# Sum of two weight blocks made by accumulating DMAs instead of VectorE, in a one-core encoder kernel

## The chip, the cores and the metric

The kernel runs on one core of one Trainium2 chip. The core has a matrix engine (TensorE, "PE" in the profile), a vector engine (VectorE, "DVE"), a scalar engine (ScalarE, "ACT"), a general engine (GpSimd, "POOL") and a synchronisation engine (SyncE, "SP"). Each of them runs its own list of instructions in order and waits for the others by semaphores. Weights come from DRAM by DMA; a DMA is issued from the queue of SP, ACT or POOL. The metric is the device time of one execution in microseconds; the median of several executions is compared.

## What is computed

A bidirectional encoder trunk of two layers on 512 positions of width 1024, in float32:

```python
for l in range(DEPTH):
    xn = rms_norm(x, ln1[l])
    z = xn @ w_in[l]
    a_q, a_i, a_ff, a_fb, a_g, b_u, b_v, c_q, c_k, c_v, gz = jnp.split(z, offsets, axis=-1)
    ...
    gates = jax.nn.sigmoid(gz.reshape(bsz, s_len, N_BRANCH, D_MODEL))
    merged = (gates[:, :, 0] * (y_a @ w_br[l, 0])
              + gates[:, :, 1] * (y_b @ w_br[l, 1])
              + gates[:, :, 2] * (y_c @ w_br[l, 2]))
    x = x + merged @ w_out[l]
    hn = rms_norm(x, ln2[l])
    x = x + jnp.square(jax.nn.relu(hn @ w_up[l])) @ w_down[l]
return rms_norm(x, final_norm)
```

The three branches are a gated linear recurrence (y_a), a gated spatial mixing (y_b) and a windowed attention (y_c).

## The kernel before

**Split products.** Every float32 matrix product is made of three faster ones. `wsplit` (L201 to L205) casts a weight tile of 128 x 1024 to a rounded high half on ScalarE (`wh`, L203), and takes the remainder on VectorE (`wl`, L204). There are `WB = 3` buffers of each. TensorE then multiplies high by high, high by low and low by high.

**Block units.** Fourteen large products are made by a scheme with seven block products in place of eight. Such a unit multiplies a left operand of 512 x 1024 by weights of 1024 x 1024, both cut in 2 x 2 blocks. Per layer there are three units of the input projection (key `un`, u = 0 to 2: the values of branches A and B, then the gates of branches C and A) and four of the down projection (key `dn`, qd = 0 to 3, between the up projections of the MLP). In order of time they are numbered here from 0: units 0 to 2 are `un` of layer 0, 3 to 6 `dn` of layer 0, 7 to 9 `un` of layer 1, 10 to 13 `dn` of layer 1.

`uload` (L187 to L195) loads a unit's eight weight tiles of 512 KB from SyncE's queue into the eight buffers `wq` (`NQ = 8`), in the order b11, b12, b22, b21, two tiles each. A buffer is loaded again only when the unit before has done with it. The four sums of weight blocks are made in place:

- b12 + b22 in `early_sums` (L417 to L420), on VectorE, ahead of the unit. The result stands in b12's buffers and is called `t3` in the unit. Where a `mark` is given, the additions are not issued before that instruction.
- b11 + t3 at L447, for the products n = 6;
- b11 - b22 at L449, for n = 5;
- b21 + b11 at L451, for n = 4.

`seven` (L422 to L475) runs the products in the order 1, 2, 6, 7, 5, 4, 3 (in unit 7: 1, 7, 6, 2, 5, 4, 3, with four other products between the first two). Product 1 needs b11, 2 needs b21, 6 needs b11 + t3, 7 needs t3 itself, and 3 needs b22. For each product two tiles are split and 24 matmuls of 512 columns run (L433 to L435). Its names in the profile are tA, tB, tC for unit 0 and 7, gA to gC for the gate units, dA to dC for the down projection. The outcomes are taken from PSUM by VectorE and ScalarE (L478 and L841 to L891).

**Order.** The program is written in one order, with priorities (`hp`, `later`). A planner then fixes the list of each engine, by its own times for the instructions. What the list holds is run in order. GpSimd's list holds the reciprocal square roots of the norms (L270, L278, L949), the stores of the gates (`thd`, L874) and of x (`xspill`, L1232), and several loads. The left operands' sums and splits (`left_x`, L407 to L415) and the sums of squares of x (`norm_sums`, L303 to L308) run in unit 0 beside the first products.

**Start.** The first loads are x, the four tiles of `bu` and unit 0's eight tiles, then eight rows of x for `norm_sums` (L777).

Of the kernel before, what the change touches and what calls it, by code (L numbers as in the profile page):

```python
# [9 lines left out]
AF = mybir.ActivationFunctionType  # L10
ALU = mybir.AluOpType
# [22 lines left out]
def _chunk_keys():  # L34

    res = []
    for l in range(DEPTH):

        res += [(l, "bu", i) for i in range(4)]


        res += [(l, "un", u, q, i) for u in range(3) for q in range(4) for i in range(2)]
        for h in range(NH):
            res += [(l, "f", h, 0), (l, "f", h, 1), (l, "q", h)]
        res += [(l, "ck"), (l, "cv")] + [(l, "cq", j) for j in range(4)]
        for d in range(KT):
            res += [(l, "gz", d)] + [(l, "yb", d // 2)] * (d % 2 == 0)
        res += [(l, "ag", h) for h in range(NH)]
        res += [(l, "y", br, fl, i) for br in (2, 0) for fl in range(2) for i in range(2)]
        res += [(l, "wo", fl, i) for fl in range(2) for i in range(4)]  # L50
        for qd in range(4):
            res += [(l, "up", qd, f) for f in range(8)]
            res += [(l, "dn", qd, q, i) for q in range(4) for i in range(2)]
    return res


CHUNK = {k: i for i, k in enumerate(_chunk_keys())}


def trunk(tc, xT, xt, ws, vec, fnb, bsb, snk, wst, rope, cmask, amask, ident, out):  # L60
    nc = tc.nc
# [33 lines left out]
    def nm(s):  # L95
        ctr[0] += 1
        return f"{s}_{ctr[0]}"

    def T(tag, name, dt=F32):
        where = part[HOME[tag]] if tag in HOME else sb  # L100
        return where.tile([P, S], dt, tag=tag, bufs=SLOTS[tag], name=nm(name))

    def begin(which):
        part[which] = pool(name=nm(which), bufs=1)
# [82 lines left out]
    def uload(*key):  # L187

        raw = []
        for i in range(8):  # L190
            t = part["wq"].tile([P, CW], F32, tag="wq", bufs=NQ, name=nm("wq"))
            with hp():
                nc.sync.dma_start(t, ws[CHUNK[key + (i // 2, i % 2)]])
            raw.append(t)
        return [raw[2 * q:2 * q + 2] for q in range(4)]  # L195

    def whl():
        return (sb.tile([P, CW], F32R, tag="wh", bufs=WB, name=nm("wh")),
                sb.tile([P, CW], F32R, tag="wl", bufs=WB, name=nm("wl")))
# [12 lines left out]
    def proj(xs, name, *key, bank="m"):  # L212

        return proj_w(xs, name, wload(*key), bank=bank)
# [88 lines left out]
    def norm_sums(n, xrows):  # L303

        ss = SM("ss8", 8)
        for j, x in enumerate(xrows):
            nc.scalar.activation(T("jk", "jk"), x, AF.Square, scale=D ** -0.5, accum_out=ss[:, j:j + 1])
        n.rc = rstd_d(ss, 0, 4)  # L308
# [94 lines left out]
    def behind(mark):  # L403

        return tc.issue_after(mark.ins) if mark else contextlib.nullcontext()
# [8 lines left out]
            res.append(h)  # L414
        return res  # L415

    def early_sums(raw, mark=None):  # L417
        with behind(mark):
            for b12, b22 in zip(raw[1], raw[2]):
                nc.vector.tensor_tensor(b12, b12, b22, ALU.add)  # L420

    def seven(raw, hs, name, on, order=(1, 2, 6, 7, 5, 4, 3), between=None, apart=False, swap=False):  # L422

# [334 lines left out]
    raw, hi, lo = sb.tile([P, CW], F32, tag="wr", bufs=WR, name=nm("wr")), *whl()  # L758
# [27 lines left out]
    for l in range(DEPTH):  # L786
# [25 lines left out]
        def project_bu():  # L812
            pts = proj_four(xs, "bu", l, "bu", banks="mmcc" if l else "mmaa")
            if l == 0:
                raw = [T("l2", "bu") for _ in pts]
                for t, pt in zip(raw, pts):
                    nc.scalar.copy(t, pt)
                return raw
            norm_rows(n1)
            return [evac(pt, "l2", "bu") for pt in pts]  # L820
# [5 lines left out]
        hx = left_x(n1, lambda: T("xs", "xs", F32R))  # L826
        if l == 0:
            raw = unit0
            early_sums(raw)
            norm_sums(n1, x0r)  # L830
            boost[0] = True
        rc = n1.rc
# [37 lines left out]
        def on_gate(i):  # L870
            w = {}

            def keep(z, t, fl):
                nc.gpsimd.dma_start(thd[:, i * 4 + t, fl * S:(fl + 1) * S], z)  # L874

            def on(which, p, pt):
                A, V = nc.scalar, nc.vector
                if which in ("P1", "P16", "P7"):
                    w[which, p] = T("zt", "zt")
                    kept.append(A.copy(w[which, p], pt))  # L880
                elif which == "P1653":
                    z = T("zt", "zt")
                    A.activation(z, pt, AF.Tanh, scale=sc[:, 4 + p:5 + p])
                    keep(z, p, 1)
                else:
                    z = w.pop(({"P2": "P1", "P165": "P7", "P74": "P16"}[which], p))
                    past.append(V.tensor_tensor(z, z, pt, ALU.add))
                    t, fl, c = {"P2": (p, 0, p), "P165": (2 + p, 1, 6 + p), "P74": (2 + p, 0, 2 + p)}[which]
                    A.activation(z, z, AF.Tanh, scale=sc[:, c:c + 1])
                    keep(z, t, fl)  # L890
            return on  # L891

        for u in range(3):
            nxt = uload(l, "un", u + 1) if u < 2 else None
            if u == 0:
                if l:
                    seven(raw, hx, "t", on_tok, (1, 7, 6, 2, 5, 4, 3), lambda mark: bu.extend(project_bu()), swap=(u + l) % 2)
                else:
                    seven(raw, hx, "t", on_tok, (1, 2, 6, 7, 5, 4, 3), swap=(u + l) % 2)
            else:  # L900
                seven(raw, hx, "g", on_gate(u - 1), between=None if l or u > 1 else rows_behind, swap=(u + l) % 2)
                if l == 0 and u == 1:
                    with behind(kept[0]):
                        for ts in (vt, bv):
                            for i, t in enumerate(ts):
                                nc.scalar.activation(t, t, AF.Copy, scale=rc[:, i:i + 1])
            if nxt:
                early_sums(nxt)
            raw = nxt
        end("G")  # L910
        end("wq")
# [332 lines left out]
        for qd in range(4):  # L1244
            hs, nh = [], [0]

            def new():
                nh[0] += 1
                return T("jk" if nh[0] == 1 else "rb" if nh[0] == 2 else "h", "sh", F32R)

            def keys(j):
                return [(l, "up", qd, 2 * j + i) for i in range(2)]

            early = {j: pair_load(keys(j), True) for j in AHEAD[qd]}
            for j in range(4):
                if j in PAIRS[qd] or j in early:
                    us = up_pair(*(early.get(j) or pair_load(keys(j), False)), hx, "s" if j % 2 else "m")
                for i in range(2):
                    f = 2 * j + i
                    if j in PAIRS[qd] or j in early:  # L1260
                        u = us[i]
                    else:
                        pt = proj(n2.xs, f'up{qd}', l, "up", qd, f, bank="s" if f % 4 > 1 else "m")
                        u = T("z", "u")
                    if f == 0:
                        raw = uload(l, "dn", qd)
                    with hp():
                        if j not in PAIRS[qd] and j not in early:
                            nc.scalar.activation(u, pt, AF.Relu)
                            mark = nc.scalar.activation(u, u, AF.Square)  # L1270
                        if f % 2 == 0:
                            hs.append(left_first(new, u))
                        else:
                            rest = left_second(new, hs[-1], u, f == 7)
                    if f == 3:
                        early_sums(raw, mark)

            def between(mark):
                for part_ in rest:
                    with hp():  # L1280
                        part_(lambda: T("l2", "sh", F32R))

            if qd == 3:
                if last:
                    for fl in range(2):
                        fn_t.append(T("z", "fn"))
                        nc.sync.dma_start(fn_t[fl], bass.AP(tensor=fnb.tensor, offset=fnb.offset + fl * S, ap=[[0, P], [1, S]]))
                else:
                    nxt = uload(l + 1, "un", 0)
            down(qd, raw, hs, xr, r2, nr2, done, between, last)  # L1290
        if not last:
            with hp():
                n1.end()
            raw = nxt
            end("mlp")
            begin("G")
            early_sums(raw)
        xsrc = xspill

    for p in reversed(pools):  # L1300
# [119 lines left out]
```

## Time and profile before

| what | us |
|---|---|
| median of 3 executions | 1645.49 |
| lowest and highest | 1645.30 and 1646.45 |
| profiled execution: its span, first to last instruction | 1644.4 |

For the profiled execution the profile gives the span and no time of its own; what lies around a span is seen by holding it against the median. The mean granted clock of TensorE was 0.999.

How to read the lines below. A group of instructions is shown as line, engine, operation, `written<-read`, shape, `xcount | busy us, mean ns | idle us just before, and what ended it`. In a list of waits each row says who waited for whom, the total, the number of times and the longest. A row of the timeline starts with its start and its duration in us. A table of stretches gives the busy time of each engine in each stretch (with the number of instructions), the granted clock, the share of the 16 DMA engines that was busy, and GB/s. "DMA to landing" is the time from the issue of a DMA to the arrival of its data. An engine's name with a q is its queue: it issues or waits.

### The profile page before, as it was taken

Reading aid. Unit: us, or ns where it says so; the run is one execution under the profiler, and the core shown is the slowest. Engines: PE = TensorE matmul, PEld = TensorE weight load, DVE = VectorE, ACT = ScalarE, POOL = GpSimd, SP = SyncE. Lnnn points to the kernel's source line nnn. Section 1 sums busy time; section 2 is a strip of 40 time slices with the busy share of each in tenths; the row PEclk is TensorE's granted clock in tenths of the full one; section 3 lists DMA queues with packets and bytes.
Section 4 is the critical chain, followed back from the end, with each engine's and each line's share of the span. In section 5 each row is a group of like instructions: output and inputs, shape, how many; then the busy total and the mean of one; then the engine's idle time right before and its main releaser. Section 6 shows DMA issues by size and latency. Waiting matters only on the chain. (4 is left out here: it accounts for less than half of the span.)

```text
span 1644.4 us, 24323 instructions
## 1 busy us (share of the span) xinstructions
PE 1631.2 (99%) x9137; PEld 1376.8 (84%) x9137; DVE 1358.9 (83%) x2183; ACT 1012.9 (62%) x1731; POOL 102.4 (6%) x165
## 2 busy tenths in 40 slices
PE   9999999999999999999999999999999999999998
PEld 7788888888888898989888888888887888989896
DVE  7888979677758988898989869887877589898887
ACT  7667567677247564646666555886862464647374
POOL 0012000000300000000010110000003000000001
PEclk9999999999999999999999999999999999999999
DMA  8343222222625333232423432223226343232311
GB/s 309 102 154 125 78 90 73 102 97 85 236 92 190 100 106 103 103 115 91 141 90 125 144 121 78 77 91 105 92 86 232 106 162 117 89 128 77 129 65 52
DMA packets 55590, 191.55 MB, mean 116 GB/s; under 512 B 7376, under 2 KB 7632, under 8 KB 55472
## 3 DMA queue, kind: packets, MB, share of 16 engines
q1 hardware_dynamic: 44352, 154.43, 27.3%
q0 software_dynamic: 10688, 35.00, 5.8%
q8 instruction: 72, 1.18, 0.3%
q10 hardware_dynamic: 432, 0.55, 0.1%
q14 instruction: 46, 0.38, 0.1%
HBM read 173.18 MB, written 16.78 MB: 116 GB/s over the span
## 5 line engine op out<-in xcount | busy, mean ns | idle before, releaser
L203 ACT CAST wh<-wq 128x1024 fp32r<-128x1024 f32 x214 | 225.2, 1053 | 205.1 <-PE dA L434 60.9
L204 DVE TENSOR_TENSOR wl<-wq,wh 128x1024 fp32r<-128x1024 f32 x214 | 260.4, 1221 | 62.8 <-ACT wh L203 60.3
L203 ACT CAST wh<-wr 128x1024 fp32r<-128x1024 f32 x164 | 172.0, 1049 | 155.1 <-PE wo L251 27.5
L204 DVE TENSOR_TENSOR wl<-wr,wh 128x1024 fp32r<-128x1024 f32 x164 | 199.9, 1220 | 61.0 <-ACT wh L203 55.1
L210 PE MATMUL up<-xh,wl 128*128 128x512 f32 x320 | 124.8, 390 | 0.0
L209 PE MATMUL up<-xl,wh 128*128 128x512 f32 x320 | 124.8, 390 | 0.0
L208 PE MATMUL up<-xh,wh 128*128 128x512 f32 x320 | 124.6, 391 | 0.0
L434 PE MATMUL dA<-wh,sh 128*128 128x512 f32 x256 | 99.8, 390 | 0.0
L433 PE MATMUL dA<-wh,sh 128*128 128x512 f32 x256 | 98.5, 390 | 0.0
L435 PE MATMUL dA<-wl,sh 128*128 128x512 f32 x256 | 91.9, 389 | 0.0
L656 DVE TENSOR_TENSOR ex<-ex 128x512 f32<-128x512 f32 x112 | 74.9, 686 | 3.5 <-ACT kt L647 3.2
L208 PEld LDWEIGHTS up<-xh,wh 128*128 128x128 f32 x320 | 60.1, 188 | 12.4
L210 PEld LDWEIGHTS up<-xh,wl 128*128 128x128 f32 x320 | 60.1, 188 | 12.3
L209 PEld LDWEIGHTS up<-xl,wh 128*128 128x128 f32 x320 | 60.1, 188 | 12.2
L644 ACT ACTIVATE qt<-ex 128x512 f32<-128x512 f32 x56 | 37.9, 677 | 33.8 <-DVE ex L656 31.8
L433 PEld LDWEIGHTS dA<-wh,sh 128*128 128x128 f32 x256 | 48.1, 188 | 10.0
L434 PEld LDWEIGHTS dA<-wh,sh 128*128 128x128 f32 x256 | 48.1, 188 | 9.9
L435 PEld LDWEIGHTS dA<-wl,sh 128*128 128x128 f32 x256 | 48.1, 188 | 9.9
L523 PE MATMUL us<-xs,wh 128*128 128x256 f32 x192 | 54.1, 283 | 0.0
L522 PE MATMUL us<-xs,wh 128*128 128x256 f32 x192 | 54.1, 283 | 0.0
L524 PE MATMUL us<-xs,wl 128*128 128x256 f32 x192 | 53.4, 283 | 0.0
L208 PE MATMUL gz<-xh,wh 128*128 128x512 f32 x128 | 50.9, 398 | 0.0
(435 smaller groups left out, 4780.6 us busy)
## 6 DMA issues: line engine op xcount, KB each, us to landing
wr<-in_ws_dram SPq DMA_DIRECT2D x158, 512.0 KB, 3.5
wq<-in_ws_dram SPq DMA_DIRECT2D x124, 512.0 KB, 4.3
thd<-zt POOLq DMA_DIRECT2D x32, 256.0 KB, 2.5
gt<-thd POOLq DMA_DIRECT2D x32, 256.0 KB, 3.9
mgd<-mg POOLq DMA_DIRECT2D x16, 256.0 KB, 2.3
mB<-mgd POOLq DMA_DIRECT2D x16, 256.0 KB, 6.7
x<-in_xT_dram SPq DMA_DIRECT2D x8, 256.0 KB, 7.5
xt<-in_xt_dram SPq DMA_DIRECT2D x8, 256.0 KB, 8.3
```

The source lines that it names most:

```text
L203: nc.scalar.copy(hi, raw)
L204: nc.vector.tensor_tensor(lo, raw, hi.bitcast(F32), ALU.subtract)
L208: nc.tensor.matmul(pt, whi, xhi, start=first, stop=False)
L209: nc.tensor.matmul(pt, whi, xlo, start=False, stop=False)
L210: nc.tensor.matmul(pt, wlo, xhi, start=False, stop=last)
L433: nc.tensor.matmul(pt, xh[:, t], hi[:, c], start=start and k == 0, stop=False, skip_group_check=True)
L434: nc.tensor.matmul(pt, xl[:, t], hi[:, c], start=False, stop=False, skip_group_check=True)
L435: return nc.tensor.matmul(pt, xh[:, t], lo[:, c], start=False, stop=k == 3, skip_group_check=True)
L522: nc.tensor.matmul(pt, hi[:, c], xh, start=n in (1, 2, 7) and k == 0, stop=False, skip_group_check=True)
L523: nc.tensor.matmul(pt, hi[:, c], xl, start=False, stop=False, skip_group_check=True)
L524: nc.tensor.matmul(pt, lo[:, c], xh, start=False, stop=k == 3, skip_group_check=True)
L656: nc.vector.tensor_tensor(o_ap, o_ap, ap_of(ex, i_, [[istep, 2]] + z), ALU.add)
```

## The change

`early_sums` no longer adds on VectorE. It issues two DMAs from GpSimd's queue, each of which reads a tile of b22 from DRAM and adds it onto the loaded tile of b12. The tiles of b22 are still loaded by `uload` too, since the products 5 and 3 use them. The function now takes the key of the unit in place of a mark; the four calls stay where they were, and the down units' sums have no mark any more. That is 28 instructions of VectorE less and 28 DMAs of 512 KB more.

```diff
-    def early_sums(raw, mark=None):
-        with behind(mark):
-            for b12, b22 in zip(raw[1], raw[2]):
-                nc.vector.tensor_tensor(b12, b12, b22, ALU.add)
+    def early_sums(raw, *key):
+        for i in range(2):
+            nc.gpsimd.dma_start(raw[1][i], ws[CHUNK[key + (2, i)]], accum_op=ALU.add)
...
-            early_sums(raw)
+            early_sums(raw, 0, 'un', 0)
...
-                early_sums(nxt)
+                early_sums(nxt, l, 'un', u + 1)
...
-                            mark = nc.scalar.activation(u, u, AF.Square)
+                            nc.scalar.activation(u, u, AF.Square)
...
-                        early_sums(raw, mark)
+                        early_sums(raw, l, 'dn', qd)
...
-            early_sums(raw)
+            early_sums(raw, l + 1, 'un', 0)
```

## Prediction

> **What bounds the kernel now.** I began with the head of the page, then asked for the waits of TensorE (PE), then for busy time in stretches that I chose around the block units.
>
> ```profile
> span 1644.4 us, 24323 instructions
> PE 1631.2 (99%) x9137; PEld 1376.8 (84%) x9137; DVE 1358.9 (83%) x2183; ACT 1012.9 (62%) x1731; POOL 102.4 (6%) x165
> ```
>
> PE is busy for 1631.2 of 1644.4 us; 13.2 us are left. VectorE (DVE) at 83% is the second engine. What a lighter DVE can give is what PE waits for it:
>
> ```profile
> PE idle L167 <- DVE idle L164: 1.6, 1, 1.6
> PE tA L435 <- DVE wl L204: 1.3, 1, 1.3
> PE wo L251 <- DVE mgl L259: 0.4, 2, 0.3
> PE po L1084 <- ACT sc L1074: 0.4, 1, 0.4
> PE av L728 <- DVE st L712: 0.3, 1, 0.3
> PE tC L435 <- DVE wl L204: 0.3, 1, 0.3
> PE kT L701 <- DVE own L634: 0.3, 1, 0.3
> PE gA L435 <- DVE wl L204: 0.2, 1, 0.2
> PE mT L1159 <- DVE gt L1174: 0.2, 1, 0.2
> ```
>
> Columns: who waited for whom, total, times, longest. The nine sum to 5.0 us. The first, 1.6, is the start of the program. The rows at L435 are inside block units: tA and tC in unit 0 (1.3 + 0.3) and gA in a gate unit (0.2), so 1.8 us in all.
>
> ```profile
> core 0: us, PE busy (x) PEld busy (x) DVE busy (x) ACT busy (x) POOL busy (x), PEclk, DMA share, GB/s
> 10.00:30.00 20.00, 20.00 (x89) 16.35 (x88) 17.62 (x24) 15.03 (x24) 1.79 (x3) 1.00 1.03 414
> 28.20:66.50 38.30, 36.70 (x160) 29.57 (x159) 34.04 (x47) 27.26 (x46) 5.10 (x3) 1.00 0.51 169
> 540.00:579.00 39.00, 39.00 (x174) 32.30 (x173) 34.75 (x44) 18.63 (x22) 0.00 (x0) 1.00 0.36 116
> ```
>
> The last row is a down-projection unit of the MLP: PE 39.00 of 39.00 us at granted clock 1.00, DVE 34.75. DVE is nearly full there, yet PE never stops: relief buys nothing. The row from 28.20 is unit 0: PE lacks 1.6 us of 38.3. The row from 10.00 is the start, where the DMA engines are full (share 1.03, 414 GB/s).
>
> **The change, part by part.** *Removed:* the two VectorE additions of each of 14 units, at L420.
>
> ```profile
> L420 DVE TENSOR_TENSOR wq<-wq,wq 128x1024 f32<-128x1024 f32 x28 | 34.2, 1223 | 13.3 <-DMA wq<-in_ws_dram 13.1
> L874 POOL DMA_DIRECT2D thd<-zt x32 | 17.5, 547 | 188.5 <-ACT zt L889 179.6 <-ACT zt L883 8.3
> ```
>
> That is 28 x 1.223 = 34.2 us of DVE busy time, and 13.3 us of DVE idling ahead of them for the load of b22. DVE falls to about 1325 us (81%). It is not on the path except through the 1.8 us above. How much of that goes? The longest wait has its own chain:
>
> ```profile
> 43.20 0.19 ACT L307 ACTIVATION_READ_ACCUMULATOR jk<-xt 128x1 f32 x1
> 45.00 4.03 POOL L278 TENSOR_TENSOR rs<-ms,mhalf_t 128x4 f32<-128x4 f32 x1 [14.10 <-DVE ms L276]
> 49.06 0.17 DVE L835 TENSOR_SCALAR gsc<-rs 128x4 f32<-128x4 f32 x1 [0.94 <-POOL rs L278]
> 51.69 0.50 PE L435 MATMUL tA<-wl,xs 128*128 128x512 f32 x1 [1.30 <-DVE wl L204]
> ```
>
> GpSimd (POOL) takes its reciprocal square root at 45.00, DVE waits for it at 49.06, and the weight halves for 51.69 stand behind that. With 2 x 1.22 us less DVE work ahead, the root could start at about 43.4 (ScalarE's last sum ends at 43.39) instead of 45.00: 1.6 us sooner, enough for the 1.3. Whether it does depends on where the planner puts it, so I take half of 1.8: **-0.9 us**.
>
> *Added:* 28 DMAs of 512 KB from POOL, each reading b22 again from DRAM and adding it onto the loaded b12. POOL's issue of a DMA lasts 0.547 us (L874): 28 x 0.55 = 15 us on an engine busy for 6%. Cover: POOL's own idle time; if that is gone, POOL's stores and square roots queue behind an accumulate. No row shows an accumulate's landing. Nearest rows:
>
> ```profile
> wq<-in_ws_dram SPq DMA_DIRECT2D x124, 512.0 KB, 4.3
> mB<-mgd POOLq DMA_DIRECT2D x16, 256.0 KB, 6.7
> DMA to landing us min/median/max: 3.3/4.3/12.8
> ```
>
> The lower end is 3.3 us, the fastest plain load of a unit's block (it can't be below nothing: the same bytes come again). The upper end is 27 us: the slowest POOL read, 6.7 us for 256 KB, twice for the size and twice for reading the destination too. I take the row of the same size and source, 4.3, plus a second pass at 414 GB/s (0.52 MB, 1.3 us) and the issue, 0.55: **about 6 us**, the second 0.6 us later. Both ends stay in the range.
>
> *The wait.* The sum b12 + b22 is first read on DVE at L447. Issue and landing of b12 (two loads), then the start of L447, for units 0, 1, 8 and 4 (a down unit):
>
> ```profile
> L193 SPq DMA_DIRECT2D wq<-in_ws_dram x2: 327/328/328, 12.0 to 12.6; - x2
> DMA to landing us min/median/max: 8.2/8.5/8.8
> 25.18 1.22 DVE L447 TENSOR_TENSOR wq<-wq,wq 128x1024 f32<-128x1024 f32 x1
> ```
>
> ```profile
> L193 SPq DMA_DIRECT2D wq<-in_ws_dram x2: 327/328/328, 51.7 to 53.4; - x2
> DMA to landing us min/median/max: 4.4/4.5/4.6
> 67.43 1.23 DVE L447 TENSOR_TENSOR wq<-wq,wq 128x1024 f32<-128x1024 f32 x1
> ```
>
> ```profile
> L193 SPq DMA_DIRECT2D wq<-in_ws_dram x2: 327/328/328, 866.8 to 868.5; - x2
> DMA to landing us min/median/max: 4.2/4.4/4.7
> 882.29 1.22 DVE L447 TENSOR_TENSOR wq<-wq,wq 128x1024 f32<-128x1024 f32 x1
> ```
>
> ```profile
> L193 SPq DMA_DIRECT2D wq<-in_ws_dram x2: 328/328/328, 566.4 to 567.6; - x2
> DMA to landing us min/median/max: 5.0/5.1/5.2
> 614.24 1.22 DVE L447 TENSOR_TENSOR wq<-wq,wq 128x1024 f32<-128x1024 f32 x1
> ```
>
> From the first b12 in place to L447: 25.18 - 20.2 = 5.0 us in unit 0, 67.43 - 56.1 = 11.3 in unit 1, 882.29 - 871.0 = 11.3 in unit 8, 614.24 - 571.4 = 42.8 in unit 4. Against 6 us, three are covered. A late sum would hold DVE at L447, and behind it stand the low halves of the next weights (L204) and the evacuations, for which PE waits. PE's own cover is the weights already split: WB is 3 pairs, so two ahead, each feeding 12 matmuls of 39.00 / 174 = 0.224 us (the down unit's row): 2 x 12 x 0.224 = 5.4 us.
>
> *Unit 0 and the full DMA engines.* The accumulates start at about 20 us, inside the stretch of share 1.03. They bring 1.05 MB, 2.5 us at 414 GB/s, or 5.1 us if the destination is read through the same engines. Behind them is b21, which PE needs next:
>
> ```profile
> 16.36 1.57 SPq L193 DMA_DIRECT2D wq<-in_ws_dram x2
> DMA to landing us min/median/max: 12.6/12.6/12.6
> 30.84 1.07 ACT L203 CAST wh<-wq 128x1024 fp32r<-128x1024 f32 x1
> 33.64 0.39 PE L433 MATMUL tB<-wh,xh 128*128 128x512 f32 x1
> ```
>
> b21 lands at 16.36 + 12.6 = 29.0, is cast at 30.84 and used at 33.64. Cast and first use are 1.73 us apart beyond the cast's 1.07. A landing at 31.5 starts the cast 0.7 us late: hidden. A landing at 34.1 starts it 3.3 us late: 3.3 - 1.7 = 1.6 us of PE. I take the first for the sum: 0.
>
> The Trainium skill, page "DMA: Bandwidth & Descriptors", section "Issuing engines are not separate DMA queues", says that DMAs from SP, ACT and POOL run on the same 16 engines and interleave; the share of 1.03 at the start fits that. Its section "Rules for kernel authors" says an accumulating DMA reads its destination and writes it later; no row here shows one. By the two together the sum would be the 5.1 us case, +1.6 instead of 0.
>
> *The sum* against the profiled execution: -0.9 + 0 = a span of 1643.5 us. The median shown, 1645.49, lies 1.1 us over the span of 1644.4, so 1645.49 - 0.9 = **1644.6 us**.
>
> **Rivals.**
>
> *All of PE's waits go (faster).* The instruction order comes from a planner; 28 DVE instructions less shift it everywhere. If every wait after the start went, 5.0 - 1.6 = 3.4 us: 1642.1. For it: seven of those eight are on DVE. Against: five of them lie outside the units, where nothing is removed. A new order can as well lose as much.
>
> *The start pays (no change).* The 5.1 us case: 1645.49 + 1.6 = 1647.1. For it: share 1.03. Against: b21 is already queued when the accumulates come.
>
> *A slow accumulate (slower).* With a landing L, DVE waits at L447 and PE loses what goes over 5.4 us: L - 10.4 in unit 0, L - 16.7 in units 1 and 8. It decides from L = 13.7, where unit 0 alone costs 3.3 us. At L = 20: 9.6 + 3.3 + 3.3 = 16.2 us, 1661.7. For it: the loads beside it in unit 0 took 8.2 to 12.6 us, and the upper end is 27. Against: POOL's 256 KB transfers land in 2.5 to 6.7 us elsewhere.
>
> *The accumulate isn't issued when b12 lands (slower, little).* POOL runs in order; an accumulate may stand behind a store that waits for ScalarE, or hold a square root (L949) behind its own wait for a load. Price: about one plain landing, 4.3 us, in one place: 1649.8. For it: in layer 1 POOL has stores and roots between each other. Against: POOL idles 94% of the time.
>
> **How the numbers follow.** About 0.2%, 3.3 us, is what a measurement of this kernel can tell from no change. Forecast 0.50 (same). Start pays 0.13 (same). All waits go 0.15: it lies on the bound, so 0.09 faster and 0.06 same. Slow accumulate 0.17 and late issue 0.05, both slower. Faster 0.09, same 0.69, slower 0.22. The range runs from 1641.0, a little beyond the second case, to 1656.0, which is the slow case with L between 17 and 18 (unit 0 alone 7, units 1 and 8 about 1 each, 9 in all, then 1.6 of the start); beyond it I leave 0.12, below it 0.04.
>
> **What would show it.** Right: L420 as 28 POOL issues with landings near 6 us, DVE busy near 1325 us, tA L435 gone or shorter among PE's waits, no wait of DVE L447 for a DMA outside unit 0. Start pays: a PE wait at tB near 34 us. Slow: DVE L447 waiting for the accumulate in units 1 and 8, PE waiting for L204 there. Wrong altogether: landings over 14 us, or waits outside the units that grew by more than 3 us.

## The result and the profile after

| | median, us | lowest and highest | executions |
|---|---|---|---|
| before | 1645.30 | 1645.01 and 1646.45 | 5 |
| after | 1656.79 | 1655.75 and 1657.20 | 5 |

The ratio is 1.0067, with a 95% interval from 1.0055 to 1.0080: the kernel became slower by about 11 us. The forecast was no change, 1644.6 us, and the upper end of the range, 1656.0, lies just below the median.

The head of the page of after:

```profile
span 1655.4 us, 24402 instructions
PE 1634.5 (99%) x9137; PEld 1377.8 (83%) x9137; DVE 1333.8 (81%) x2155; ACT 1013.4 (61%) x1731; POOL 120.6 (7%) x193
```

The span grew by 11.0 us. TensorE runs the same 9137 instructions, but is busy for 3.3 us more (1634.5 against 1631.2) and idle for 7.7 us more (20.9 against 13.2). The waits of TensorE say where it idles; columns are who waited for whom, the total, the times and the longest:

```profile
PE tA L432 <- ACT wh L203: 3.7, 1, 3.7
PE tB L432 <- ACT wh L203: 3.1, 2, 1.7
PE idle L167 <- DVE idle L164: 1.6, 1, 1.6
PE tA L434 <- DVE wl L204: 1.2, 1, 1.2
```

Lines have moved up by one: L432 to L434 are the matmuls of the units, and b11 += t3 is L446. Three of the four rows carry tA and tB. In the timeline their four waits lie in unit 0: at tB 1.4 us ahead of 34.51 and 1.7 ahead of 39.60, at tA 3.7 ahead of 46.65 and 1.2 ahead of 49.91. Their 8.0 us stand where before had 1.6 (tA 1.3 and tC 0.3). The stretches around them, columns as in the prediction:

```profile
core 0: us, PE busy (x) PEld busy (x) DVE busy (x) ACT busy (x) POOL busy (x), PEclk, DMA share, GB/s
30.00:40.00 10.00, 6.89 (x28) 4.72 (x28) 3.88 (x7) 4.77 (x10) 0.00 (x0) 1.00 1.01 359
40.00:50.00 10.00, 5.05 (x17) 2.99 (x15) 8.14 (x14) 7.69 (x19) 1.04 (x1) 0.77 0.07 23
47.60:55.70 8.10, 6.91 (x17) 4.86 (x16) 8.07 (x10) 3.04 (x3) 0.00 (x0) 0.50 0.00 0
50.00:60.00 10.00, 10.00 (x33) 7.96 (x34) 7.79 (x9) 3.89 (x6) 0.00 (x0) 0.72 0.30 104
```

After the wait of 3.7 us the granted clock is 0.50 from 47.6 to 55.7 us. In TensorE's timeline the 17 matmuls there start 0.427 us apart, against 0.227 before: 17 x 0.200 = 3.4 us, which is the busy time that TensorE gained.

The added DMAs, as a group of instructions and as issues, and the only wait for them on VectorE:

```profile
L419 POOL DMA_DIRECT2D wq<-in_ws_dram x28 | 24.4, 870 | 535.3 <-DMA wq<-in_ws_dram 402.3
wq<-in_ws_dram POOLq DMA_DIRECT2D x28, 512.0 KB, 9.5
DMA to landing us min/median/max: 5.6/9.5/12.1
DVE wq L446 <- DMA wq<-in_ws_dram: 1.8, 2, 1.5
```

They take 9.5 us in the median and 12.1 at most. GpSimd waits 402.3 us for loads in front of them, and among TensorE's longest nine waits none is for GpSimd. VectorE waits for a sum twice, 0.3 and 1.5 us, both in unit 8, and outside unit 0 no wait of TensorE has grown by more than 0.4 us. So the transfers are slower than estimated and covered nearly everywhere. In unit 0 something else stands out. VectorE's timeline there:

```profile
29.87 0.43 DVE L380 TENSOR_TENSOR sf<-x 128x256 f32<-128x256 f32 x1
34.49 1.23 DVE L204 TENSOR_TENSOR wl<-wq,wh 128x1024 fp32r<-128x1024 f32 x1 [4.19 <-ACT wh L203]
37.54 0.69 DVE L259 TENSOR_TENSOR xs<-sf,xs 128x512 fp32r<-128x512 f32 x1 [1.82 <-ACT xs L258]
...
42.80 0.69 DVE L259 TENSOR_TENSOR xs<-sf,xs 128x512 fp32r<-128x512 f32 x1 [1.40 <-ACT xs L258]
43.41 1.22 DVE L446 TENSOR_TENSOR wq<-wq,wq 128x1024 f32<-128x1024 f32 x1
...
47.50 1.22 DVE L446 TENSOR_TENSOR wq<-wq,wq 128x1024 f32<-128x1024 f32 x1
```

The two sums of unit 0 were issued at 19.6 and 20.9 us and landed at 29.1 and 33.0 (9.5 and 12.1 us later). Yet b11 += t3 runs at 43.41 and 47.50, 14 us after its data. VectorE idled for 4.19 us in between, for the cast of b21. It is the order of its list: in before the two additions stood at 25.18 and 30.32, between the sums of the left operand; now they stand behind the low halves of b21 (L204) and the last of left_x (L259). ScalarE's list has moved in the same way:

```profile
33.42 1.04 ACT L203 CAST wh<-wq 128x1024 fp32r<-128x1024 f32 x1 [3.81 <-DMA wq<-in_ws_dram]
36.27 0.63 ACT L307 ACTIVATE jk<-xt 128x512 f32<-128x512 f32 x1 [1.81 <-DMA xt<-in_xt_dram]
...
45.47 0.19 ACT L307 ACTIVATION_READ_ACCUMULATOR jk<-xt 128x1 f32 x1
45.56 1.03 ACT L203 CAST wh<-wq 128x1024 fp32r<-128x1024 f32 x1
```

The cast at 33.42 is b21's (landed 33.3 us, before 29.0), the one at 45.56 is that of product 6, and between them stand the eight sums of squares. The first of them waits 1.81 us for a row of x; the rows land at 36.2 to 40.8 us instead of 30.8 to 36.6. TensorE starts product 6 at 46.65 us; in before it started at 39.08 without a wait. VectorE's second addition, TensorE's start of product 6 and GpSimd's load of `cos`, first in before:

```profile
30.32 1.22 DVE L447 TENSOR_TENSOR wq<-wq,wq 128x1024 f32<-128x1024 f32 x1
39.08 0.39 PE L433 MATMUL tA<-wh,xs 128*128 128x512 f32 x1
28.63 0.54 POOL L926 DMA_DIRECT2D cos<-in_rope_dram  x1 [8.94 <-DVE sf L383]
```

and in after, where the second addition is the row of 47.50 above:

```profile
46.65 0.79 PE L432 MATMUL tA<-wh,xs 128*128 128x512 f32 x1 [3.70 <-ACT wh L203]
24.27 0.57 POOL L925 DMA_DIRECT2D cos<-in_rope_dram  x1 [2.56 <-DVE sf L383]
```

The last row shows one more thing that moved. GpSimd's loads of `cos` and `sin`, 256 KB each, follow VectorE's sums of the left operand (L383). These come earlier now that the additions are out of their way, so the two loads are issued at 24.27 and 25.00 us instead of 28.63 and 30.36, while b21 is still on its way.

What the planner holds for the landing of such a DMA isn't in the trace; the lists that it wrote are. So there are two suspects. **Theory A:** the accumulating DMAs hold the 16 DMA engines in the full start, and b21 and x come late. **Theory O:** the planner, which sees a DMA where an addition was, writes other lists in unit 0, and in those lists b11 += t3 and product 6's cast wait for work that they don't need.

### The profile page after: what moved, and what is told of

It reads as the page before. It is cut to its first block, busy times and chain, and to the rows that moved or that the text cites. A ratio compares the mean times of both kernels' runs of the same rounds, so it can differ in the third digit from the quotient of the medians.

```text
span 1655.4 us, 24402 instructions
## 1 busy us (share of the span) xinstructions
PE 1634.5 (99%) x9137; PEld 1377.8 (83%) x9137; DVE 1333.8 (81%) x2155; ACT 1013.4 (61%) x1731; POOL 120.6 (7%) x193
## 3 DMA queue, kind: packets, MB, share of 16 engines
q1 hardware_dynamic: 44352, 154.43, 27.6%
q0 software_dynamic: 14720, 49.69, 10.6%
## 5 line engine op out<-in xcount | busy, mean ns | idle before, releaser
L204 DVE TENSOR_TENSOR wl<-wq,wh 128x1024 fp32r<-128x1024 f32 x214 | 260.6, 1222 | 87.8 <-ACT wh L203 84.0
L204 DVE TENSOR_TENSOR wl<-wr,wh 128x1024 fp32r<-128x1024 f32 x164 | 200.2, 1221 | 73.9 <-ACT wh L203 66.8
L432 PE MATMUL dA<-wh,sh 128*128 128x512 f32 x256 | 98.7, 389 | 0.0
L434 PE MATMUL dA<-wl,sh 128*128 128x512 f32 x256 | 92.1, 389 | 0.0
L419 POOL DMA_DIRECT2D wq<-in_ws_dram x28 | 24.4, 870 | 535.3 <-DMA wq<-in_ws_dram 402.3
L434 PEld LDWEIGHTS dA<-wl,sh 128*128 128x128 f32 x256 | 48.1, 188 | 10.0
L432 PEld LDWEIGHTS dA<-wh,sh 128*128 128x128 f32 x256 | 48.0, 188 | 10.0
```

Of the source, the lines that this page charges most:

```text
L204: nc.vector.tensor_tensor(lo, raw, hi.bitcast(F32), ALU.subtract)
L432: nc.tensor.matmul(pt, xh[:, t], hi[:, c], start=start and k == 0, stop=False, skip_group_check=True)
L434: return nc.tensor.matmul(pt, xh[:, t], lo[:, c], start=False, stop=k == 3, skip_group_check=True)
```

## The experiments

Every ratio is to the kernel before on the same chip; intervals are 95%.

### Which unit: all but unit 0, and unit 0 alone

```diff
+            if key == (0, 'un', 0):
+                nc.vector.tensor_tensor(raw[1][i], raw[1][i], raw[2][i], ALU.add)
+                continue
```

> The changed kernel, with unit 0's two sums back on VectorE: 26 accumulating DMAs, 2 additions. Theory S (the whole loss is made at the start, in unit 0, where the DMA engines are full): within 0.2% of the kernel before, 1642 to 1649 us; accumulates of the other units still land about 9 us after issue and nothing waits for them. Rival R (accumulates cost a little in every unit, or the new instruction order does): most of the loss stays, 1653 to 1657 us.

```diff
+            if key != (0, 'un', 0):
+                with behind(mark):
+                    nc.vector.tensor_tensor(raw[1][i], raw[1][i], raw[2][i], ALU.add)
+                continue
...
```

> The kernel before, with unit 0's two sums alone made by accumulating DMAs: 2 DMAs, 26 additions. Theory S: the whole loss is here, 1653 to 1660 us, with TensorE waiting near 34, 39 and 46 us and its clock below 1 after that. Rival R: two of 28 DMAs cost little, 1645 to 1649 us.

With unit 0 back on VectorE and 26 DMAs in the other 13 units, the time is 1646.14 us (before 1645.58), ratio 1.0002 [0.9993, 1.0011]. With unit 0 alone by DMA it is 1655.55, ratio 1.0059 [1.0045, 1.0073], with TensorE's waits of after (tA 3.7, tB 1.7, tA 1.2). The whole loss comes from two of the 28 DMAs. The other 26 neither cost nor bring anything that can be measured.

### The transfers alone, in the order of before

The kernel before, its sums on VectorE, and four loads of 256 KB of b22 more from GpSimd's queue, into spare tiles that nothing reads, once b12 is in place. First plain, then accumulating.

```diff
...
+            for i in range(4):
+                nc.gpsimd.tensor_copy(scr[i][:, 0:1], raw[1][i // 2][:, 0:1])
+                c = slice((i % 2) * S, (i % 2 + 1) * S)
+                nc.gpsimd.dma_start(scr[i], ws[CHUNK[(0, 'un', 0, 2, i // 2)], :, c])
```

> The kernel before with all 28 additions on VectorE, and beside them plain loads from GpSimd's queue of the same two tiles of b22 into spare buffers that nobody reads, issued once b12 has landed in unit 0 (four loads of 256 KB; four small memsets and copies on GpSimd go with them). Nobody waits for them, so what they cost is contention alone. Theory S1 (bytes on full DMA engines: 1.05 MB at 414 GB/s put b21 and the rows of x back by 2.5 us): 0 to 3 us over the kernel before, 1645 to 1649. Theory S2 (the accumulate holds the engines twice as long as its bytes): this run near the kernel before, the next one well over it. Rival W (the loss comes of waiting for the sum): 1645 to 1647, and the next run too.

> As the run before it, but the four extra DMAs accumulate onto the spare buffers instead of overwriting them. Nobody waits for them. Theory S1: the same as the plain loads within 1 us. Theory S2 (read, add and write back holds the engines about twice as long): b21 lands 4 to 6 us late as in the changed kernel, 1650 to 1658 us. Rival W (waiting for the sum is what costs): 1645 to 1647 us.

Plain: 1645.94 us, 1.0002 [0.9992, 1.0011]. Accumulating: 1647.79, 1.0013 [1.0004, 1.0022], or 2.2 us. The same bytes as read-modify-write load the engines more; from 20 to 30 us the first row is the accumulating kernel, the second the plain one:

```profile
20.00:30.00 10.00, 10.00 (x46) 8.29 (x45) 9.96 (x14) 5.49 (x10) 7.29 (x10) 1.00 1.05 354
```

```profile
20.00:30.00 10.00, 10.00 (x46) 8.29 (x45) 9.43 (x14) 4.87 (x9) 4.86 (x10) 1.00 1.03 414
```

Engines as full (1.05 and 1.03), but 354 GB/s instead of 414. In unit 0 ScalarE's and VectorE's lists of both kernels are those of before. Theory A is true in kind, and gives 2 of 11 us (0.7 to 3.6 by the interval). The 1650 to 1658 us of theory S2 did not come, and neither did the late b21 that it named: b21 lands at 28.9 and 31.3 us (before 29.0 and 30.2), and TensorE waits 0.5 us at tB. So e4 does not show again what delayed b21 to 33.3 in after.

### The half clock

16 idle matmuls fill TensorE's gap ahead of product 6 in the kernel after.

```diff
...
+            if n == 2 and fill:
+                with behind(end_):
+                    pf = PT("s", "fill")
+                    for _ in range(fill):
+                        nc.tensor.matmul(pf, n1.xs[0][0][:, 0:P], n1.xs[0][0], start=True, stop=True)
...
```

> The changed kernel with 16 more matmuls of 512 columns on TensorE in unit 0, between the products 2 and 6, on operands that are there; nobody reads what they give. They add 16 x 0.227 = 3.6 us of TensorE work where the changed kernel's TensorE idles 3.7 us. Theory C (part of the loss is the clock, which the records show at 0.72 to 0.77 from 40 to 60 us after that idle stretch): the work fits in the gap, the clock stays at 1.00, and about 3 us come back: 1652 to 1655 us. Rival: the clock costs nothing that the gap would not have cost, or the matmuls only put the next product back: 1656 to 1660 us.

The granted clock from 40 to 50 us is 1.00 where after has 0.77, and the time is 1654.81, 1.0061 [1.0046, 1.0076]. That lies inside theory C's range, but it is not told from after's 1.0067 [1.0055, 1.0080]. The half clock is real in the trace; that without it most of the time is lost to other waits is a reading of it, since TensorE still waits 2.1 us at tA and 1.8 at tB there.

### Parts of the late work taken away

The sums of squares (`norm_sums`) queued behind product 6's second cast on ScalarE:

```diff
...
-            norm_sums(n1, x0r)
...
+                    with behind(marks[6]):
+                        norm_sums(n1, x0r)
...
```

> The changed kernel with the eight sums of squares of x (ScalarE, L307) queued behind the weight cast of unit 0's product 6, and their root and scales after that. The accumulates and every load stay as they are. Theory Q (ScalarE's list holds casts behind sums that wait for the late rows of x): TensorE's second wait at tB and the one of 3.7 us at tA go or shrink to 1 us, the clock stays up, 1647 to 1651 us. Rival W (the sum b12 + b22 itself is late for product 6): the wait at tA stays, 1653 to 1658 us. Rival D (b21's late landing is all): one wait of 1.5 us less or none, 1653 to 1656 us.

Four loads of constants from GpSimd's queue held back behind the norm's square root, so that they don't run beside unit 0's weights:

```diff
...
+        with behind(None if l else root[0]):
+            nc.gpsimd.dma_start(wst_t, wst[l])
+            nc.gpsimd.dma_start(bsb_t, bass.AP(tensor=bsb.tensor, offset=bsb.offset + l * 512, ap=[[0, P], [1, 512]]))
+            nc.gpsimd.dma_start(cos_t, rope[:, 0])
+            nc.gpsimd.dma_start(sin_t, rope[:, 1])
```

> The changed kernel with the four loads of 256 KB for later stages (wst, bsb, cos, sin: 1.05 MB on GpSimd's queue, issued between 17 and 26 us) put behind the root of the norm at about 46 us. Theory D (full DMA engines put b21 and the rows of x back): 1.05 MB less in the full stretch, 2.5 us at 414 GB/s: b21 lands 2 to 3 us sooner than in the changed kernel, TensorE's waits at tB and tA shrink, 1647 to 1653 us. Rival W (the sum is late by itself, or the order of instructions costs): no change, 1655 to 1658 us.

Both:

> Both edits of the two runs before: the sums of squares behind product 6's cast, and the four loads put off. If both theories Q and D hold, unit 0 is as in the kernel before or a little better: 1644 to 1648 us. If the sum itself is late (W): 1650 us or more. If it beats the kernel before, it does so by at most the 1.8 us that TensorE waited in units there.

The first: 1653.47, 1.0048 [1.0033, 1.0063]. The second: 1652.57, 1.0043 [1.0028, 1.0058]. Both: 1650.27, 1.0025 [1.0015, 1.0035]. Each step gives something back, none all, and the 1651 us or less of theory Q and the 1648 or less of both together did not come. In the first TensorE still waits 2.3 us twice at tA. The second lies in theory D's range, and b21's first tile lands at 29.2 us there, as in before, with the accumulates in place; the waits at tB shrink to 0.2 us, but that of 3.6 us at tA stays. With both, TensorE waits 1.8 us at tA and 2.2 at tC, the sums land at 29.4 and 33.2 us and the additions run at 38.44 and 40.83, still behind all of left_x.

### Plain DMAs in the same place and the same lists

In the kernel after, unit 0's two DMAs overwrite b12 with b22 and don't add; unit 0 then computes with b22 in place of the sum. VectorE's and ScalarE's lists of unit 0 are those of after.

```diff
+            if key == (0, 'un', 0):
+                nc.gpsimd.dma_start(raw[1][i], ws[CHUNK[key + (2, i)]])
+                continue
```

> The changed kernel, but unit 0's two DMAs overwrite b12 with b22 instead of adding (unit 0 then computes with b22 in place of b12 + b22; the other units accumulate as in the changed kernel). The lists of all engines stand in the same order as in the changed kernel, the waits are the same, and the bytes from DRAM too; only the read and the addition at the destination are gone. Theory A (the accumulate holds the DMA engines about twice as long as its bytes, which puts b21 and x back): most of the loss goes, 1646 to 1649 us, with b21 landed by 32 us. Rival O (the new order of the lists, or a second transfer behind the first, costs whatever it does): 1652 to 1657 us.

> The changed kernel itself, for comparison on the same chip as the run before it: 1655 to 1658 us, 1.0055 to 1.008 times the kernel before.

Plain: 1654.47, 1.0052 [1.0039, 1.0065]. After, again: 1656.12, 1.0067 [1.0053, 1.0080]. TensorE's waits with the plain DMAs:

```profile
PE tA L435 <- ACT wh L203: 3.7, 1, 3.7
PE tA L437 <- DVE wl L204: 1.2, 1, 1.2
```

The waits at tB are gone: b21 lands at 30.4 and 32.4 us, in time. The wait ahead of product 6 has stayed, 3.7 us, though the overwritten tiles are in place at 28.3 and 30.8 us. The 1646 to 1649 us of theory A did not come: without any addition in unit 0's DMAs, 9.2 of 10.8 us remain (medians less before's 1645.31), and the two intervals overlap. The bytes of the two transfers are still there in this run; beside the lists of before they cost 0.4 us (e3). So theory A falls as the main cause.

### The two edits on the kernel before

> The kernel before, without any accumulate, with the sums of squares behind product 6's cast and the four loads put off. If what these two edits gave beside the accumulates was only the repair of their damage: 1644 to 1647 us, no change. If they gain by themselves, at most the 1.6 us that TensorE waits in unit 0: 1643.5 us.

1644.48 us, 0.9994 [0.9985, 1.0003]: the two edits of e8 are worth nothing that can be told from nothing where no accumulate is. TensorE's waits in unit 0 are all gone there. It has the lowest median of all kernels here, but is not shown to be faster.

### The new order without any DMA

The kernel before, nothing transferred that before doesn't transfer; only unit 0's b11 += t3 is queued on VectorE behind the last operation of left_x. Both lists of unit 0 then come out nearly as in after, the casts of product 6 behind the eight sums of squares among it.

```diff
...
-                        V.tensor_tensor(b11[i], b11[i], t3[i], ALU.add)
+                        with behind(six):
+                            V.tensor_tensor(b11[i], b11[i], t3[i], ALU.add)
...
-                    seven(raw, hx, "t", on_tok, (1, 2, 6, 7, 5, 4, 3), swap=(u + l) % 2)
+                    seven(raw, hx, "t", on_tok, (1, 2, 6, 7, 5, 4, 3), swap=(u + l) % 2, six=tail[0])
```

> The kernel before, all sums on VectorE and no transfer added; only unit 0's two additions b11 += t3 are queued on VectorE behind the last operation of left_x. ScalarE's and VectorE's lists of unit 0 then stand nearly as in the kernel after: product 6's casts behind the eight sums of squares and behind b21's casts. Theory O (the new order of the in-order lists is the main cost): PE waits 2 to 5 us ahead of product 6 of unit 0 (tA, on ACT wh), the granted clock falls there, and the time is 1649 to 1654 us. Rival C (the data are late because the transfers contend, the order alone costs little): PE's waits in unit 0 stay under 1.5 us and the time is 1644.5 to 1647.5.

1650.48 us (before 1645.58), 1.0029 [1.0018, 1.0039]. TensorE's waits, the timeline of VectorE and TensorE, and the stretch:

```profile
PE tA L435 <- ACT wh L203: 4.5, 1, 4.5
```

```profile
40.79 0.69 DVE L259 TENSOR_TENSOR xs<-sf,xs 128x512 fp32r<-128x512 f32 x1 [0.43 <-ACT xs L258]
41.40 2.35 DVE L450 TENSOR_TENSOR wq<-wq,wq 128x1024 f32<-128x1024 f32 x2
```

```profile
43.74 0.80 PE L435 MATMUL tA<-wh,xs 128*128 128x512 f32 x1 [4.53 <-ACT wh L203]
```

```profile
40.00:50.00 10.00, 6.20 (x14) 4.40 (x15) 9.57 (x15) 5.13 (x10) 1.04 (x1) 0.68 0.00 0
```

The trace is after's in small: the additions late at 41.40, product 6 at 43.74 instead of 39.08, the clock down to 0.68. The order alone makes the wait, and costs 4.9 us. For this part of the 11 us theory O is shown, not only argued.

### The change with a repaired list

The kernel of e8, and left_x's last pieces queued on VectorE behind b11 += t3; the DMAs stay. First the pieces 2 and 3, then piece 3 alone.

```diff
...
+            def sums(mark, k=k, h=h):
+                with behind(mark):
+                    left_sums(new, h, n.xf[k], n.xf[k + 4])
+            if parts is not None and k > 1:
+                parts.append(sums)
...
-                        V.tensor_tensor(b11[i], b11[i], t3[i], ALU.add)
+                        mark = V.tensor_tensor(b11[i], b11[i], t3[i], ALU.add)
+                        if parts:
+                            parts.pop(0)(mark)
...
```

> The kernel of e8 (the change with the sums of squares behind product 6's second cast and four constant loads deferred), with left_x's pieces 2 and 3 queued on VectorE behind unit 0's two additions b11 += t3, so that these stand directly behind b21's low halves. The DMAs are those of e8. Theory O: the additions start within 2 us of the later of the sum's landing (29.4 and 33.2 in e8) and b21's second low half (about 35), PE's wait ahead of product 6 falls from 1.8 to under 1 us and the time from 1650.3 to 1645.5 to 1648. Rival C: the time stays that of e8, 1649 to 1651.5, since b21 and the x rows are as late as there.

1652.02 us, 1.0038 [1.0025, 1.0050]: a miss. The wait ahead of product 6 is gone, but the moved pieces come late themselves, and TensorE waits for them instead (tA on DVE xs 1.8, tC on ACT wh 1.0, tC on DVE wl 1.0, and 0.5 more). A list was mended in one place and broken in another.

```diff
-            if parts is not None and k > 1:
+            if parts is not None and k > 2:
...
-                        if parts:
+                        if parts and i == 0:
```

> As e13, but only left_x's piece 3 is queued on VectorE behind unit 0's first addition b11 += t3; piece 2 keeps its place ahead of b21's low halves. In e13 the wait ahead of product 6 was gone, but the moved left-hand pieces made later products wait 4.3 us (tC 1.0 and 1.0, tA 1.8). Theory O: the additions start by 36 and 39 us, PE's waits in unit 0 sum to under 2 us, and the time is 1645.5 to 1648.5 us, that is e4's cost of the contention (2 us) or less. Rival C: it stays at 1650 to 1652, as e8 and e13.

1646.08 us, 1.0002 [0.9993, 1.0011]. TensorE's waits, the longest two of the first 130 us, and VectorE's and TensorE's rows:

```profile
PE idle L167 <- DVE idle L164: 1.6, 1, 1.6
PE tC L442 <- ACT wh L205: 1.2, 1, 1.2
```

```profile
34.73 1.22 DVE L456 TENSOR_TENSOR wq<-wq,wq 128x1024 f32<-128x1024 f32 x1
...
37.67 1.22 DVE L456 TENSOR_TENSOR wq<-wq,wq 128x1024 f32<-128x1024 f32 x1
```

```profile
38.79 0.39 PE L442 MATMUL tA<-wh,xs 128*128 128x512 f32 x1
```

All 28 accumulating DMAs are there and unit 0's sums land as late as in after (29.5 and 33.2 us), and product 6 starts at 38.79 with no wait. Nothing that can be measured is left of the 11 us. Two things share in that: the edits of e8, with which b21 lands at 28.9 and 32.4 us here instead of 33.3 and 35.8 and ScalarE's casts come first, and the order of VectorE's list. Against before on the same chip each time, 10.8 us (e10) became 4.2 with the edits of e8 and 0.4 with the list mended as well. No run mends the list without the edits of e8.

### The sum of them

| us more than before | lists of before | lists of after |
|---|---|---|
| nothing transferred | 0 | 4.9 (e12) |
| plain DMAs in unit 0 | 0.4 (e3) | 9.2 (e9) |
| accumulating DMAs in unit 0 | 2.2 (e4) | 10.8 (e10) |

The order costs 4.9 us by itself, the transfers 2.2. Together they cost 3.7 us more than the sum of both. A reading for this that no run separates: in the lists of after the additions and the casts stand behind everything that b21 and x bring, so each microsecond by which those are late goes through; in the lists of before there is room. The lists of after also bring `cos` and `sin` into b21's way, at 24.27 and 25.00 us; in e12, e3 and e4 `cos` is issued at 27.7 us or later, and with the four loads put off (e7) b21's first tile lands as in before. e3 and e4 transfer in pieces of 256 KB behind a small copy, and e12's lists are nearly those of after, not wholly; the split is to be read to a microsecond or two.

## Why the prediction was wrong, step by step

- **The step that failed: "The wait"**, with its slack of 5.0 us from b12 in place to L447. It was measured between the landing and the place that L447 has in the list of before, and the change's cost was then worked out as if a late sum would hold VectorE at that place ("L - 10.4 in unit 0"). The planner moved the addition: from 25.18 and 30.32 to 43.41 and 47.50 us, and product 6's cast with it. By the formula the measured landings, 9.5 and 12.1 us, cost 0 and 1.7 us; after lost 11. e12 shows that the new place costs 4.9 without any late sum, and e14 that behind a better list the late sum costs nothing that can be measured.
- **"Unit 0 and the full DMA engines", taken as 0.** b21's first tile landed at 33.3, not at 31.5, and the sign named for this rival came: TensorE's waits at tB, 3.1 us, the first at 34.5. The working held for that tile: by it a landing at 33.3 costs 0.7 us (33.3 - 30.84 - 1.73), and product 2 began 0.87 us later than in before (34.51 against 33.64). It left out the second tile, whose cast stood behind a sum that waited for x and cost another 1.7 us. That b21 was queued 4 us ahead of the accumulates, the prediction's reason against, did not keep it from being late. But the accumulates alone did not do it: b21 lands at 28.9 in e4 and at 29.2 in e7. The price of 1.6 is near e4's 2.2 us by luck, since only 0.5 us of waiting at tB is in that run.
- **The Trainium skill**, page "DMA: Bandwidth & Descriptors", section "Rules for kernel authors": that an accumulating DMA reads its destination and writes it later. The trace agrees as far as a trace can: 354 against 414 GB/s with full engines (e4, e3). The prediction weighed the 5.1 us case by it and then took the cheaper one.
- **The landing of "about 6 us"** was 9.5 in the median and 12.1 at most; the issue 0.87 us, not 0.55. Both lie inside the bounds, 3.3 to 27, and neither decided: 13 units at these landings cost nothing (e1).
- **-0.9 us from a lighter VectorE** did not come. The square root was to start at 43.4 us; in after it starts at 45.94, later than in before (45.00), since ScalarE's last sum of squares ends at 45.66. The tA wait on VectorE in after (1.2 us, ahead of 49.91) is another one, in product 6. e1 can't test this term, since it leaves unit 0's additions on VectorE.
- **VectorE "near 1325 us"** came to 1333.8. The durations of its instructions, summed over all groups, did fall by about 34.6 us (1486.5 to 1451.9). But busy time counts it once where two instructions overlap, and this overlap fell too, from 127.6 to 118.1 us. Durations can't be taken off a busy time one for one.
- **"All of PE's waits go"** was priced as a gain from a new order, with the remark that a new order can as well lose as much. That remark was the right rival: its mechanism, the place of the addition that reads the sum, should have had a price of its own, 4.9 us in e12.
- **"A slow accumulate"** (from L = 13.7) did not occur, 12.1 being the longest; of its signs only VectorE's wait in unit 8 came, 1.8 us, and no wait of TensorE followed. Nor did **"the accumulate isn't issued when b12 lands"**: unit 0's were issued at 19.6 and 20.9, as b12 landed, and unit 8's first 0.9 us after it. The range missed by 0.8 us, and its upper end came from the slow accumulate, not from what happened. Neither sign of "wrong altogether" came, landings over 14 us or longer waits outside the units: the prediction looked for its error in the wrong places.

## What to carry to other kernels

Where a planner writes the lists, a changed instruction is not only its own cost: it moves whoever reads its outcome, and slack measured in the old list is not slack in the new one. Before relying on such slack, look at which unrelated work the reader may fall behind, above all in the start where data come late; after the run, compare the order of the lists first, and the durations second. Here 26 additions taken from an engine that isn't the bound brought nothing (e1), and the DMAs in their place share the DMA engines with the loads.

## What the runs showed of the hardware

- **An accumulating DMA took nearly twice the DMA engines' time of a plain load here.** The queues of before, then of after (packets, MB, share of 16 engines' span):

```profile
q1 hardware_dynamic: 44352, 154.43, 27.3%
q0 software_dynamic: 10688, 35.00, 5.8%
```

```profile
q1 hardware_dynamic: 44352, 154.43, 27.6%
q0 software_dynamic: 14720, 49.69, 10.6%
```

  q0 grew by 14.69 MB, the bytes of 28 reads of 0.52 MB, and from 5.8% of 1644.4 to 10.6% of 1655.4 us, by 80.1 us: 2.9 us of all engines each. q1's plain loads take 27.6% of 1655.4 us for 154.43 MB, 1.55 us for as many bytes, and q0's plain transfers in before take about 1.4 (5.8% of 1644.4 us for 35.00 MB).
- **The clock fell behind one wait of 3.7 us, and behind two shorter ones.** In after it was 0.50 behind one wait of 3.7 us. In e8 it fell as well, behind two waits of 1.8 and 2.2 us with 1.2 us of matmuls between them (40.84 to 42.06); TensorE's timeline, then the stretch:

```profile
40.84 0.50 PE L436 MATMUL tA<-wh,xs 128*128 128x512 f32 x1 [1.83 <-ACT wh L205]
...
41.66 0.40 PE L437 MATMUL tA<-wh,xs 128*128 128x512 f32 x1
44.20 0.80 PE L436 MATMUL tC<-wh,xs 128*128 128x512 f32 x1 [2.15 <-ACT wh L205]
```

```profile
40.00:50.00 10.00, 7.01 (x18) 5.22 (x19) 9.01 (x9) 8.44 (x18) 0.00 (x0) 0.66 0.00 1
```

  In e13 a wait of 1.8 us by itself left it at 1.00. The Trainium skill, page "TensorE: Matmul & The Clock Gate", section "HAM oscillation — how this bites in real kernels", gives the rule "no PE-idle gaps >~3.4µs"; after agrees with it, and in e8 the clock fell though neither gap is that long.
